# A two-layer decoder trunk on one core: retention transposes held back, output weights laid elsewhere, the start of x reordered

## The chip, the core and the metric

The kernel runs on one core of a Trainium2 chip. The time is that of one execution on the device in microseconds (us), the median of several executions. TensorE is called PE here, VectorE DVE, ScalarE ACT, GpSimd POOL and SyncE SP; nearly all transfers are issued by SP.

## The reference

The trunk has two layers over a sequence of 2048 rows with 1024 columns. Each layer is `x <- x + RMSNorm_post(mixer(RMSNorm_pre(x)))`. The mixer of layer 0 feeds one input projection to retention (4 heads, chunks of 128 rows, rotary q and k) and to stick-breaking attention (8 heads); the mixer of layer 1 feeds HGRN2 (4 heads) and an RG-LRU behind a causal convolution. Each path is multiplied by its own SiLU gate, the two are put side by side, and one output projection follows. The part of retention that the change touches is, for a chunk:

```
scores = einsum('bhnid,bhnjd->bhnij', qc, kc) * decay
o_intra = einsum('bhnij,bhnje->bhnie', scores, vc)
chunk_kv = einsum('bhnjd,hj,bhnje->nbhde', kc, k_decay, vc)
```

and afterwards an RMS norm over each head of `o_intra + o_inter`.

## The kernel before

The sequence is worked in two halves of 1024 rows: layer 0 half 0, layer 0 half 1, layer 1 half 0, layer 1 half 1. Each of these four steps has a mixer (`stick` for layer 0, which contains the retention; `hgrn` for layer 1, which contains the LRU), and an `out_phase` that multiplies the mixed columns by `w_out`, adds x and prepares the transposed input of the next step. The place where a mixer's last projection ends on PE and the first matmul of `out_phase` begins is called a seam here. There are four seams; in the profiled execution they lie near 505, 1260, 1720 and 2189 us.

Every float32 matmul with 512 columns is made of three products of a high and a low part: a weight piece `raw` is loaded by SP, ACT casts it to `wh` (`load_w`, L131), DVE takes the rest to `wl` (L132), and PE multiplies (wh, xh), (wh, xl) and (wl, xh). `w_out` of one column half (`c`) comes in four such pieces, q0 to q3, of two row blocks each. The mixed columns of half a sequence are written to memory (`mixd`) by the mixers, except the last 512 wide block of each of the two groups `g` of 512 rows, which goes straight to the tiles `mh` and `ml` (`mix_direct`, L218 and L219). The stored ones come back as one tile `mr` for each of eight blocks of 128 rows (`mix_rows`, load L225), which ACT casts to `mh` (L227) and DVE to `ml` (L228). The block with number 0 is called row 0, and so on.

In `stick` the last work before the seam is `ret_gate` for head 3, once for g=0 and once for g=1: 24 matmuls into a PSUM tile `pp`, a sigmoid `sg` on ACT (L296), and the two products on DVE, L297 (`ro` times `sg`) and L298 (times `pp`). In `hgrn` the last work is `lg_proj(3)`, likewise with a sigmoid (L198) and two products on DVE (L204, L777).

The retention of one chunk runs as side work between other matmuls (`weave` and `mixed` deal out matmuls by nanoseconds that the generators yield). Its steps on PE are the scores (L328), the transposes of k (L334), the products with v and the state (L344, L345), the k-v products (L350), and at the end four transposes of the normed result `rst` (L361), which need `rs`, a root computed by POOL (L71), and DVE's product L357. `late` with `later`, `tick` and `flush` is a list of postponed functions with due times in nanoseconds of PE work.

Each engine works through its own list of instructions in the order in which the program gives them to it, after the scheduler's priorities; a tile that takes over memory of an older tile waits for the older one's last reader.

## Time and profile before

| | |
|---|---|
| median of 3 runs | 2286.71 us (2285.96 to 2290.03) |
| profiled execution | 2291.48 us, of which the span of its instructions is 2289.6 us |
| PE | 97% of the span busy |
| DVE, ACT, POOL | 61%, 48%, 31% |
| PE before its first matmul | 9.39 us |

The span is the time from the first to the last instruction on the core. A line of the timeline gives the start, the duration, the engine, the line of the kernel and what is written from what, and in brackets how long the engine had been idle before and what ended that. Matmuls overlap: their listed duration is about 0.39 us, while they start 0.227 us apart when nothing is waited for.

### The profile page before, as it was taken

The page shows a single profiled execution, that of the slowest core. Times are in us where ns is not written, and L with a number is a line of the kernel's source. Part 1 is how long each engine was busy: PE and PEld are TensorE (multiplying, and loading weights), DVE is VectorE, ACT ScalarE, POOL GpSimd, SP SyncE. Part 2 cuts the span into 40 slices and gives each one's busy share as a digit, 9 for nine tenths or more (in the row PEclk, how much of TensorE's full clock was granted, in tenths as well). Part 3 has the DMA queues.
Part 4 walks back from the last instruction along what each step waited for, and adds up shares of the span by engine and source line. Part 5 has one row for each costly group of instructions (what it writes and reads, how often), then busy time and mean ns, then how long its engine had stood idle before and what let it go on. Part 6 is the DMA issues. An engine that isn't in the chain of part 4 may idle for free.

```text
span 2289.6 us, 31620 instructions
## 1 busy us (share of the span) xinstructions
PE 2213.7 (97%) x11392; PEld 1805.6 (79%) x11392; DVE 1390.7 (61%) x2049; ACT 1099.4 (48%) x2192; POOL 706.0 (31%) x992
## 2 busy tenths in 40 slices
PE   7999999999999999999999999999999999999998
PEld 6888877777888888788777887877877877878777
DVE  5545567674567677888898554655555535455543
ACT  5334456553455666777776433243245323433331
POOL 0322244421044344665664001222240013122300
PEclk9999999999999999999999999999999999999999
DMA  6443334246433222213323641111116511111161
GB/s 191 112 124 97 111 104 120 86 132 208 160 103 104 65 74 79 79 50 91 88 58 103 213 151 38 42 38 37 52 50 212 190 47 33 42 37 42 51 221 74
DMA packets 236092, 223.69 MB, mean 98 GB/s; under 512 B 21280, under 2 KB 181408, under 8 KB 235936
## 3 DMA queue, kind: packets, MB, share of 16 engines
q1 hardware_dynamic: 235776, 221.15, 31.4%
q8 instruction: 90, 1.47, 0.3%
q14 instruction: 66, 0.54, 0.1%
q0 software_dynamic: 160, 0.52, 0.1%
HBM read 148.22 MB, written 52.43 MB: 88 GB/s over the span
## 4 chain that ended last, share of the span: by engine, by line
PE 78%; DVE 10%; ACT 4%; DMA 3%; issue 3%; POOL 2%; SPq 0%; POOLq 0%; DVEq 0%; ACTq 0%
PE pp L152 42%; PE pp L640 5%; PE o L640 4%; PE o L515 4%; PE z L640 4%; PE tr L500 4%; PE z L474 2%; DVE a L487 2%; PE z L473 2%; PE z L894 2%; PE tr L112 1%; DMA xr<-in_x 1%; PE z L747 1%; DVE wl L132 1%; DVE wtl L505 1%
## 5 line engine op out<-in xcount | busy, mean ns | idle before, releaser
L152 PE MATMUL pp<-xh,wh 128*128 128x512 f32 x1664 | 687.5, 413 | 0.6 <-ACT xh L114 0.6
L152 PE MATMUL pp<-xh,wl 128*128 128x512 f32 x1664 | 658.1, 396 | 0.0
L152 PE MATMUL pp<-xl,wh 128*128 128x512 f32 x1664 | 656.5, 395 | 0.0
L152 PEld LDWEIGHTS pp<-xh,wl 128*128 128x128 f32 x1664 | 313.4, 188 | 67.7 <-issue 1.4
L490 POOL TENSOR_TENSOR b<-b,a 128x511 f32<-128x511 f32 (+2 forms) x320 | 316.2, 988 | 161.9 <-DVE a L487 96.1
L152 PEld LDWEIGHTS pp<-xh,wh 128*128 128x128 f32 x1664 | 314.3, 189 | 53.9 <-ACT xh L114 1.0
L152 PEld LDWEIGHTS pp<-xl,wh 128*128 128x128 f32 x1664 | 315.1, 189 | 49.3 <-issue 0.5
L487 DVE TENSOR_TENSOR_SCAN a<-a,past 128x512 f32<-128x512 f32 x192 | 244.5, 1275 | 76.6 <-ACT a L477 74.4
L477 ACT ACTIVATE a<-z 128x512 f32<-128x512 f32 (+2 forms) x320 | 172.4, 539 | 235.7 <-PE z L474 197.1
L132 DVE TENSOR_TENSOR wl<-raw,wh 128x1024 fp32r<-128x1024 f32 x136 | 171.1, 1264 | 141.9 <-ACT wh L131 139.6
L131 ACT CAST wh<-raw 128x1024 fp32r<-128x1024 f32 x136 | 142.8, 1053 | 194.1 <-PE pp L152 168.2
L71 POOL TENSOR_TENSOR rs<-rs,mhalf 128x1 f32<-128x1 f32 (+1 forms) x96 | 67.0, 698 | 515.3 <-DVE rs L70 506.6
L505 DVE TENSOR_TENSOR wtl<-tr,wth 128x512 fp32r<-128x512 f32 (+1 forms) x320 | 190.1, 595 | 39.0 <-ACT wth L504 38.0
L504 ACT CAST wth<-tr 128x512 fp32r<-128x512 f32 (+1 forms) x320 | 169.5, 530 | 62.9 <-PE tr L500 61.0
L500 PE MATMUL tr<-ident,b 128*128 128x128 f32 x1088 | 176.1, 276 | 11.8 <-DVE wtl L505 10.7
L500 PEld LDWEIGHTS tr<-ident,b 128*128 128x128 f32 x1088 | 133.5, 141 | 59.1 <-DVE wtl L505 17.6
L478 ACT ACTIVATE b<-z 128x512 f32<-128x512 f32 (+2 forms) x320 | 171.0, 534 | 0.0
L482 DVE TENSOR_TENSOR_SCAN a<-a,past 128x128 f32<-128x128 f32 (+3 forms) x128 | 104.5, 817 | 85.0 <-ACT a L477 84.6
L515 PE MATMUL o<-wth,v 128*128 128x512 f32 (+1 forms) x320 | 128.1, 400 | 0.2 <-ACT mol L521 0.2
L866 POOL TENSOR_TENSOR kg<-kg,t 128x256 f32<-128x256 f32 x96 | 71.1, 740 | 173.2 <-PE z L894 108.0
L480 POOL TENSOR_SCALAR_AFFINE_SELECT b<-b 128x128 f32<-128x128 f32 x128 | 44.2, 345 | 259.6 <-ACT b L478 251.2
L473 PE MATMUL z<-k,qh 128*128 128x512 f32 (+2 forms) x320 | 118.6, 371 | 1.3 <-DMA k<-kd 0.6
(216 smaller groups left out, 3610.3 us busy)
## 6 DMA issues: line engine op xcount, KB each, us to landing
raw<-in_even_w_in SPq DMA_DIRECT2D x56, 512.0 KB, 3.9
raw<-in_odd_w_in SPq DMA_DIRECT2D x48, 512.0 KB, 3.8
xr<-in_x SPq DMA_DIRECT2D x32, 512.0 KB, 4.2
xr<-x1d SPq DMA_DIRECT2D x32, 512.0 KB, 4.5
mr<-mixd SPq DMA_DIRECT2D x32, 448.0 KB, 4.8
qh<-qrh SPq DMA_DIRECT2D x64, 128.0 KB, 2.3
ql<-qrl SPq DMA_DIRECT2D x64, 128.0 KB, 2.4
x1d<-y SPq DMA_DIRECT2D x16, 512.0 KB, 2.9
```

What stands on the lines that cost most here:

```text
L132: nc.vector.tensor_tensor(out=wl, in0=raw, in1=wh.bitcast(F32), op=ALU.subtract)
L152: nc.tensor.matmul(ps, w[:, k, :], xx[g][:, k, :], start=(n == 0), stop=(n == 3 * KD - 1))
L473: nc.tensor.matmul(z[:, 0:n], qh[:, tcol], K[e, c][:, 0:n], start=True, stop=False)
L477: nc.scalar.activation(out=A[:, 0:n], in_=z[:, 0:n], func=AF.Sigmoid, scale=-0.125)
L478: nc.scalar.activation(out=B[:, 0:n], in_=z[:, 0:n], func=AF.Sigmoid, scale=0.125)
L487: nc.vector.tensor_tensor_scan(out=A[:, ::-1], data0=A[:, ::-1], data1=past[:, 0:1].to_broadcast([128, 512]), initial=carry[ti][:, 0:1], o ...
L490: nc.gpsimd.tensor_tensor(out=B[:, 0:n - 1], in0=B[:, 0:n - 1], in1=A[:, 1:n], op=ALU.mult)
L500: nc.tensor.transpose(tr[:, ti * 128:ti * 128 + 128], bt[ti][:, sj * 128:sj * 128 + 128], ident)
L504: nc.scalar.copy(out=wh[:, cols], in_=tr[:, cols])
L505: nc.vector.tensor_tensor(out=wl[:, cols], in0=tr[:, cols], in1=wh[:, cols].bitcast(F32), op=ALU.subtract)
L515: nc.tensor.matmul(O[:, cols], V[e, c][:, sj, :], w[:, cols], start=(diag and sj == 0 and w is wh), stop=(c == 0 and sj == 3 and w is wl))
L640: nc.tensor.matmul(ps, m[g][:, k, o:o + 128], w[:, k % 2, :], start=(n == 0), stop=(n == 3 * KD - 1))
```

## The change

Five parts, in the order of the diff:

1. The `tick` of the list `late` runs any entry that is due, not only the first. The four transposes at the end of a retention chunk, the copy behind them and the store of `ro` are packed into a function `turn`. It is called right behind the scores of the next chunk, or when 9000 ns of PE work have passed, whichever comes first; after the last chunk of a call, at once.
2. At the start of the program row block 0 of x is loaded first, then the identity, then row blocks 1 to 3, then the norm weights; the constant tile `past` is built after the projections of the first pair.
3. Row 0 of the mixed columns of layer 1 is no longer loaded through the weight tiles `raw` ahead of the others, but through the two buffers `mr` of the pool `o2`, as the others.
4. The first two pieces of `w_out` (q0, q1) get a pool of their own, `w2a`, on the other end of the on-chip memory. In layer 1 the LRU's scratch pool `lru1` is given up before `lg_proj(3)`, and the pieces are loaded there; in layer 0 the pool is opened in `out_phase`. The pool `w2` has two buffers where it had four.
5. POOL's product of gate and convolution in the LRU (L755) is made in two halves of 512 columns.

```diff
@@ -22,8 +22,9 @@
 KD = D // 128
 EPS = 1e-6
 LAG = 2
+RET_LAG = 9000
 SHIFT = 1
-EARLY = (0, 1)
+EARLY = (0, 0)
 LEVELS = (2, 4, 8, 16, 32, 64)
 
 
@@ -48,10 +49,7 @@
         return (o_bank[-1] if tag == "o" else ps_p).tile([128, 512], F32, tag=tag, name=tag)
 
     ident = const.tile([128, 128], F32, name="ident")
-    nc.sync.dma_start(out=ident, in_=a["c_ident"])
     pre_w = const.tile([128, 2, KD], F32, name="pre_w")
-    for i in range(2):
-        nc.sync.dma_start(out=pre_w[:, i, :], in_=a["pre_norm_w"][i].rearrange("(k p) -> p k", p=128))
     mhalf = const.tile([128, 4], F32, name="mhalf")
     nc.vector.memset(mhalf, -0.5)
     state = const.tile([128, 512], F32, name="state")
@@ -162,8 +160,9 @@
     def tick(ns):
         for item in late:
             item[0] -= ns
-        while late and late[0][0] <= 0:
-            late.pop(0)[1]()
+        for item in [i for i in late if i[0] <= 0]:
+            late.remove(item)
+            item[1]()
 
     def run(gen):
         for ns in gen:
@@ -315,6 +314,12 @@
         lo, hi = slice(0, 64), slice(64, 128)
         nc.gpsimd.memset(q[hi, 0], 0.0)
         nc.gpsimd.memset(q[lo, 1], 0.0)
+        held = []
+
+        def release():
+            if held:
+                held.pop()()
+
         for ch in chunks:
             gg, o = half * 2 + ch // 4, (ch % 4) * 128
             v = p.tile([128, 4, 128], F32, tag="rv", bufs=2, name="rv")
@@ -327,6 +332,7 @@
             for h in range(4):
                 nc.tensor.matmul(sc[:, h, :], k[:, h // 2, :], q[:, h % 2, h // 2, :], start=True, stop=True)
             yield 860
+            release()
             st = p.tile([128, 4, 128], F32, tag="rst", name="rst")
             nc.vector.tensor_tensor(out=st, in0=sc, in1=decay, op=ALU.mult)
             ktp = bank("tr")
@@ -355,14 +361,18 @@
                                                in1=kvp[:, pr, :], op0=ALU.mult, op1=ALU.add)
             rs = rms_heads([st[:, h, :] for h in range(4)], kt[:, 0:128], 4)
             nc.vector.tensor_tensor(out=st, in0=st, in1=rs.unsqueeze(2).to_broadcast([128, 4, 128]), op=ALU.mult)
-            yield 0
-            pt = bank("tr").rearrange("p (h t) -> p h t", h=4)
-            for h in range(4):
-                nc.tensor.transpose(pt[:, h, :], st[:, h, :], ident)
+
+            def turn(st=st, gg=gg, o=o):
+                pt = bank("tr").rearrange("p (h t) -> p h t", h=4)
+                for h in range(4):
+                    nc.tensor.transpose(pt[:, h, :], st[:, h, :], ident)
+                ot = t_p.tile([128, 4, 128], F32, tag="sg", name="rot")
+                nc.scalar.copy(out=ot, in_=pt)
+                nc.sync.dma_start(out=rod[gg][:, :, o:o + 128], in_=ot)
+            held.append(turn)
+            later(RET_LAG, lambda turn=turn: release() if held and held[0] is turn else None)
             yield 440
-            ot = t_p.tile([128, 4, 128], F32, tag="sg", name="rot")
-            nc.scalar.copy(out=ot, in_=pt)
-            nc.sync.dma_start(out=rod[gg][:, :, o:o + 128], in_=ot)
+        release()
 
     kd = [[dr_p.tile([128, 512], F32, name=f"kd{h}_{c}") for c in range(2)] for h in range(8)]
     vd = [[dr_p.tile([128, 512], F32, name=f"vd{h}_{c}") for c in range(2)] for h in range(8)]
@@ -372,11 +382,6 @@
             kv_p, qr_p, q_p, a_p, b_p, wt_p, g_p, t_p, r_p = (scope(es, n, b) for n, b in (
                 ("skv", 8), ("sqr", 2), ("sq", 2), ("sa", 6), ("sb", 9), ("swt", 3), ("sg", 3), ("stmp", 2), ("srt", 1)))
             past = scope_o(es, 1).tile([128, 512], F32, tag="past", name="past")
-            build = t_p.tile([128, 512], F32, tag="sg", name="build")
-            nc.vector.memset(build, 0.0)
-            nc.gpsimd.affine_select(out=build[:, 384:512], in_=build[:, 384:512], compare_op=ALU.is_gt, fill=1.0,
-                                    base=0, pattern=[[-1, 128]], channel_multiplier=1)
-            nc.scalar.copy(out=past, in_=build)
             D_ = [({}, {}, {}, {}) for _ in range(4)]
 
             def pair_proj(pr):
@@ -552,6 +557,11 @@
             t_att = 65000 if half else 23000
             cs = rope_tables(half, r_p)
             run(pair_proj(0))
+            build = t_p.tile([128, 512], F32, tag="sg", name="build")
+            nc.vector.memset(build, 0.0)
+            nc.gpsimd.affine_select(out=build[:, 384:512], in_=build[:, 384:512], compare_op=ALU.is_gt, fill=1.0,
+                                    base=0, pattern=[[-1, 128]], channel_multiplier=1)
+            nc.scalar.copy(out=past, in_=build)
             flush()
             def qk(*parts):
                 return ret_proj_qk(half, xT, r_p, t_p, cs, parts)
@@ -574,11 +584,27 @@
             weave(att(3), t_att, seq(side((5, 8), proj_of(1, pair_gate(3))), gate(0, 1)), 43500)
             run(gate(2, 3))
 
-    def out_phase(layer, half, M, following):
+    def piece(layer, c, q, pool):
+        order = (0, 1, 2, 4, 5, 6, 7, 3) if layer == 0 else tuple(range(8))
+        return load_w(w_out[layer][:, c * 512:(c + 1) * 512], 2, 512, pool, order[2 * q:2 * q + 2])
+
+    class first_pieces:
+        def __init__(self, layer, es, instead=None):
+            self.layer, self.es, self.instead = layer, es, instead
+
+        def __iter__(self):
+            if self.instead:
+                proj_w(1, 2560 + 3 * 128)
+                self.instead.close()
+            self.pool = scope(self.es, "w2a", 2, side="right")
+            self.made = [piece(self.layer, 0, q, self.pool) for q in range(2)]
+            return iter(())
+
+    def out_phase(layer, half, M, following, ahead, first):
         prep_row = prep_step = xT = None
         with ExitStack() as es:
             scope_o(es, 2)
-            w2_p, p2, p1, y_p = scope(es, "w2", 4), scope(es, "o2", 2), scope(es, "o1", 1), scope(es, "y", 8)
+            p2, w2_p, p1, y_p = scope(es, "o2", 2), scope(es, "w2", 2), scope(es, "o1", 1), scope(es, "y", 8)
             if following:
                 rows, prep_row, x_p = prep_rows(es, *following)
                 xT, prep_step = prep_cols(rows, following[0])
@@ -587,13 +613,12 @@
             early = EARLY[layer]
             mrs = [None] * early
             mh, ml = zip(*(mix_slot(M, g) for g in range(2)))
-            order = (0, 1, 2, 4, 5, 6, 7, 3) if layer == 0 else tuple(range(8))
-
-            def piece(c, q, pool):
-                return load_w(w_out[layer][:, c * 512:(c + 1) * 512], 2, 512, pool, order[2 * q:2 * q + 2])
-
+            if not first:
+                first = first_pieces(layer, ahead)
+                with tc.high_priority(offset=300):
+                    iter(first)
             with tc.high_priority(offset=300):
-                W = [[piece(0, q, w2_p) for q in range(4)], []]
+                W = [first.made + [piece(layer, 0, q, w2_p) for q in (2, 3)], []]
             with tc.high_priority(offset=300):
                 for tt in range(early, 8):
                     mrs.append(mix_rows(half, M, tt, p2, "mr"))
@@ -626,11 +651,11 @@
                 if c == 1:
                     if not prep_step:
                         xrs.update((tt, load_x(tt)) for tt in range(8))
-                    W[1] += [piece(1, q, w2_p) for q in (2, 3)]
+                    W[1] += [piece(layer, 1, q, first.pool) for q in (2, 3)]
                 for tt in range(8):
                     if (c, tt) == (0, 2):
                         with tc.issue_after(mrs[5]):
-                            W[1] += [piece(1, q, w_p) for q in (0, 1)]
+                            W[1] += [piece(layer, 1, q, w_p) for q in (0, 1)]
                     g, o = tt // 4, (tt % 4) * 128
                     ps = bank(("pp", "z", "o")[(c * 8 + tt) % 3])
                     n = 0
@@ -752,7 +777,8 @@
                     nc.scalar.activation(out=av, in_=r, func=AF.Exp, scale=lam8[:, j:j + 1])
                     nc.scalar.activation(out=r, in_=r, func=AF.Tanh, scale=lam4[:, j:j + 1])
                     nc.scalar.activation(out=r, in_=r, func=AF.Sqrt)
-                    nc.gpsimd.tensor_tensor(out=ig, in0=ig, in1=xc, op=ALU.mult)
+                    for x in (slice(0, 512), slice(512, 1024)):
+                        nc.gpsimd.tensor_tensor(out=ig[:, x], in0=ig[:, x], in1=xc[:, x], op=ALU.mult)
                     nc.vector.scalar_tensor_tensor(out=r, in0=av, scalar=1.0, in1=r, op0=ALU.add, op1=ALU.mult)
                     if half == 0:
                         nc.vector.memset(r[:, 0:1], 1.0)
@@ -784,9 +810,10 @@
 
         return lx_proj, lg_proj
 
-    def hgrn(es, half, xT, M):
+    def hgrn(es, half, xT, M, ahead):
         scope_o(es, 2)
-        lp1, lp5, lpg = scope(es, "lru1", 1), scope(es, "lru5", 4), scope(es, "lrug", 1)
+        scratch = ExitStack()
+        lp1, lp5, lpg = scope(scratch, "lru1", 1, side="right"), scope(es, "lru5", 4), scope(es, "lrug", 1)
         p1, p, p4 = scope(es, "hg1", 1), scope(es, "hg", 2), scope(es, "hg4", 4)
         ones = p1.tile([128, 128], F32, name="ones")
         nc.vector.memset(ones, 1.0)
@@ -931,8 +958,10 @@
         flush()
         for h in range(3):
             weave(head_scan(h), 20000, seq(head_proj(h + 1), lx_proj(h + 1)), 57000)
-        weave(head_scan(3), 20000, seq(*(lg_proj(j) for j in range(4))), 41600)
+        pieces = first_pieces(1, ahead, scratch)
+        weave(head_scan(3), 20000, seq(*(lg_proj(j) for j in range(3)), pieces, lg_proj(3)), 41600)
         flush()
+        return pieces
 
     steps = [(layer, half) for layer in range(2) for half in range(2)]
     with ExitStack() as es:
@@ -940,6 +969,11 @@
         xT, step = prep_cols(rows, 0)
         for tt in range(8):
             row(tt)
+            if tt == 0:
+                nc.sync.dma_start(out=ident, in_=a["c_ident"])
+            if tt == 3:
+                for i in range(2):
+                    nc.sync.dma_start(out=pre_w[:, i, :], in_=a["pre_norm_w"][i].rearrange("(k p) -> p k", p=128))
             if tt in (3, 5):
                 proj_w(0, 2048 if tt == 3 else 2560)
             if tt % 4 == 3:
@@ -947,6 +981,7 @@
                     step(tt // 4, k)
     for n, (layer, half) in enumerate(steps):
         M = {}
+        ahead, first = ExitStack(), None
         if layer == 0:
             stick(half, xT, M)
             if half == 1:
@@ -954,8 +989,9 @@
                 odd_const()
         else:
             with ExitStack() as es:
-                hgrn(es, half, xT, M)
-        xT = out_phase(layer, half, M, steps[n + 1] if n + 1 < len(steps) else None)
+                first = hgrn(es, half, xT, M, ahead)
+        with ahead:
+            xT = out_phase(layer, half, M, steps[n + 1] if n + 1 < len(steps) else None, ahead, first)
 
 
 def _tables():
```

In the pieces of the two programs' orders below, the numbers of lines are those of each program: L131 before is L129 after, L227 is L226, L218 is L217, L296 is L295, L361 is L368, L152 is L150, L198 is L197.

ACT at the first seam of layer 0, before. `wh<-raw` are the casts of weight pieces (first x2: q0, q1; second: q2, q3), `mh<-mr` the casts of rows, `sg<-pp` the sigmoids of `ret_gate`, the last two those of head 3, for g=0 and for g=1:

```order
L131 CAST wh<-raw 128x1024 x2
L520 COPY mo<-o 64x512
L521 COPY mol<-o 64x512
L296 ACTIVATE sg<-pp 128x512 x2
L131 CAST wh<-raw 128x1024 x2
L296 ACTIVATE sg<-pp 128x512
L227 CAST mh<-mr 128x7x128
L218 CAST mh<-ro 128x512
L227 CAST mh<-mr 128x7x128
L296 ACTIVATE sg<-pp 128x512
L227 CAST mh<-mr 128x7x128
L218 CAST mh<-ro 128x512
```

The same place after the change:

```order
L295 ACTIVATE sg<-pp 128x512 x2
L226 CAST mh<-mr 128x7x128 x2
L295 ACTIVATE sg<-pp 128x512
L217 CAST mh<-ro 128x512
L226 CAST mh<-mr 128x7x128
L295 ACTIVATE sg<-pp 128x512
L226 CAST mh<-mr 128x7x128
L129 CAST wh<-raw 128x1024 x2
L217 CAST mh<-ro 128x512
L226 CAST mh<-mr 128x7x128 x2
L129 CAST wh<-raw 128x1024 x2
L226 CAST mh<-mr 128x7x128 x2
```

All four casts of weights stood ahead of the sigmoid of head 3 for g=0 and of the rows; now they stand behind the sigmoid for g=1, q0 and q1 behind row 3, and q2 and q3 behind rows 4 and 5. In the new program the cast of q0 also waits for DVE's product with that last sigmoid (the tile `sg` lay in memory that `w2a` takes over), and PE's fourth matmul of `out_phase`, which is the first of a fourth row block, for the product after it (L298 before); the loads of `raw` for q2 and q3 stand on SP behind the loads of rows 4 and 5 and wait for `wl` of q0 and q1, whose `raw` tiles they take over.

PE at the second chunk of the retention in half 0, from the attention's product that stands 2 instructions ahead of the transposes `tr<-ident,rst` before:

```order
L152 MATMUL pp<-xl,wh 128x512
L152 MATMUL pp<-xh,wl 128x512
L473 MATMUL z<-k,qh 128x256
L474 MATMUL z<-k,ql 128x256
L361 MATMUL tr<-ident,rst 128x128 x4
L152 MATMUL pp<-xh,wh 128x512
L152 MATMUL pp<-xl,wh 128x512
L152 MATMUL pp<-xh,wl 128x512
```

The same place after the change:

```order
L478 MATMUL z<-k,qh 128x256
L479 MATMUL z<-k,ql 128x256
L150 MATMUL pp<-xh,wh 128x512
L150 MATMUL pp<-xl,wh 128x512
L150 MATMUL pp<-xh,wl 128x512
L505 MATMUL tr<-ident,b 128x128 x4
L150 MATMUL pp<-xh,wh 128x512
L150 MATMUL pp<-xl,wh 128x512
L150 MATMUL pp<-xh,wl 128x512
L368 MATMUL tr<-ident,rst 128x128 x4
L520 MATMUL o<-wth,v 128x512
```

The transposes have moved behind six projection matmuls and one set of the attention's transposes.

ACT at the first seam of layer 1, before. `mh<-gt` are the direct casts of the LRU's last gate for g=0 and g=1:

```order
L198 ACTIVATE sg<-pp 128x512
L227 CAST mh<-mr 128x7x128
L218 CAST mh<-gt 128x512
L198 ACTIVATE sg<-pp 128x512
L131 CAST wh<-raw 128x1024 x2
L218 CAST mh<-gt 128x512
L131 CAST wh<-raw 128x1024 x2
L227 CAST mh<-mr 128x7x128 x2
L643 ACTIVATE y,sy<-pp 128x512
```

The same place after the change:

```order
L197 ACTIVATE sg<-pp 128x512
L217 CAST mh<-gt 128x512
L197 ACTIVATE sg<-pp 128x512
L217 CAST mh<-gt 128x512
L129 CAST wh<-raw 128x1024 x2
L226 CAST mh<-mr 128x7x128 x4
L668 ACTIVATE y,sy<-pp 128x512
```

Row 0, which was cast ahead of the gate, now stands behind the last gate's cast and the pieces q2 and q3; q0 and q1 are cast earlier and are out of this piece.

## Rows read from the trace of the kernel before

**Rows 1.** The page, part 1: busy us, share of the span, instructions.
```profile
PE 2213.7 (97%) x11392; PEld 1805.6 (79%) x11392; DVE 1390.7 (61%) x2049; ACT 1099.4 (48%) x2192; POOL 706.0 (31%) x992
```

**Rows 2.** Waits of PE: line, releaser: us in total, times, longest.
```profile
...
PE tr L361 <- DVE rst L357: 12.6, 8, 2.3
...
PE pp L640 <- ACT wh L131: 5.5, 4, 1.9
PE z L894 <- POOL kg L866: 5.2, 10, 0.7
PE pp L640 <- DVE wl L132: 4.1, 5, 1.2
PE tr L361 <- DVE wtl L505: 3.8, 5, 2.0
```

**Rows 3.** Timeline of PE, last retention chunk of each sequence half.
```profile
...
436.63 0.63 PE L361 MATMUL tr<-ident,rst 128*128 128x128 f32 x4 [1.09 <-DVE rst L357]
...
1169.80 0.63 PE L361 MATMUL tr<-ident,rst 128*128 128x128 f32 x4 [2.11 <-DVE rst L357]
```

**Rows 4.** Windows: stretch, length, busy by engine, PEclk (1.00 full), DMA share, GB/s.
```profile
...
263.60:267.00 3.40, 3.40 (x11) 2.77 (x10) 0.17 (x1) 1.07 (x2) 0.00 (x0) 0.51 0.10 33
...
1728.00:1734.80 6.80, 6.05 (x14) 4.63 (x15) 4.22 (x5) 3.61 (x5) 0.00 (x0) 0.50 0.75 234
```

**Rows 5.** Timeline of ACT: the first row block of x at the start.
```profile
...
6.58 1.06 ACT L97 ACTIVATE xn<-xr 128x1024 f32<-128x1024 f32 x1 [4.50 <-DMA xr<-in_x]
```

**Rows 6.** Timeline of ACT at the first layer-0 seam.
```profile
...
495.74 1.05 ACT L131 CAST wh<-raw 128x1024 fp32r<-128x1024 f32 x1 [0.65 <-DMA raw<-in_even_w_out]
...
504.12 0.94 ACT L227 CAST mh<-mr 128x896 fp32r<-128x896 f32 x1 [4.22 <-DMA mr<-mixd]
...
506.36 0.59 ACT L296 ACTIVATE sg<-pp 128x512 f32<-128x512 f32 x1
509.85 0.94 ACT L227 CAST mh<-mr 128x896 fp32r<-128x896 f32 x1 [2.89 <-DMA mr<-mixd]
```

**Rows 7.** Timeline of DVE at the same seam.
```profile
...
495.13 1.23 DVE L132 TENSOR_TENSOR wl<-raw,wh 128x1024 fp32r<-128x1024 f32 x1 [0.25 <-ACT wh L131]
...
505.09 1.09 DVE L228 TENSOR_TENSOR ml<-mr,mh 128x896 fp32r<-128x896 f32 x1 [3.74 <-ACT mh L227]
...
507.70 0.69 DVE L297 TENSOR_TENSOR ro<-ro,sg 128x512 f32<-128x512 f32 x1
```

**Rows 8.** Timeline of SP's DMA issues at the same seam.
```profile
...
497.40 1.51 SPq L225 DMA_DIRECT2D mr<-mixd  x2
...
506.21 8.85 SPq L225 DMA_DIRECT2D mr<-mixd  x4
```

**Rows 9.** Timeline of PE at the same seam.
```profile
...
505.11 0.50 PE L640 MATMUL pp<-wh,mh 128*128 128x512 f32 x1 [0.40 <-ACT mh L227]
```

**Rows 10.** DMA issues over the whole run: count, KB each, median us to landing.
```profile
...
mr<-mixd SPq DMA_DIRECT2D x32, 448.0 KB, 4.8
...
raw<-in_even_w_out SPq DMA_DIRECT2D x8, 512.0 KB, 5.6
...
mixd<-ro SPq DMA_DIRECT2D x12, 256.0 KB, 2.0
```

**Rows 11.** Timeline of DVE, end of the constants before the second seam.
```profile
...
1251.47 0.16 DVE L712 TENSOR_SCALAR lam<-s 128x4 f32<-128x4 f32 x1
```

**Rows 12.** Timeline of PE at the second layer-0 seam.
```profile
...
1260.21 0.39 PE L640 MATMUL pp<-wh,mh 128*128 128x512 f32 x1
```

**Rows 13.** Timeline of PE at the first layer-1 seam.
```profile
...
1721.08 0.49 PE L640 MATMUL pp<-wh,mh 128*128 128x512 f32 x1 [1.62 <-ACT wh L131]
```

**Rows 14.** Timeline of ACT at the same seam.
```profile
...
1719.50 0.60 ACT L198 ACTIVATE sg<-pp 128x512 f32<-128x512 f32 x1 [3.21 <-PE pp L152]
...
1722.09 0.61 ACT L218 CAST mh<-gt 128x512 fp32r<-128x512 f32 x1
```

**Rows 15.** Timeline of DVE at the same seam.
```profile
...
1720.85 0.69 DVE L777 TENSOR_TENSOR gt<-gt,ht 128x512 f32<-128x512 f32 x1
```

## The prediction

> **What bounds the kernel now.** I read the shares of the engines first: PE is busy 97% of the span [rows 1], so that of 2289.6 us some 76 are idle on PE, and everything else can only matter through them. Then I read what ended PE's waits [rows 2]: the transposes at the end of a retention chunk wait 12.6 us for DVE's `rst` and 3.8 us for a free `tr` bank, the first matmuls of `out_phase` wait 5.5 and 4.1 us for weights, and the HGRN's products 5.2 us for POOL. Then the granted clock in short windows: behind a wait of 2.1 us it stands at 0.51, its lower level of 1.2 GHz, for 3.4 us, and behind the longer waits of the first layer-1 seam at 0.50 for 6.8 us [rows 4]. What PE does there takes twice as long, so a stretch of 3.4 us costs 1.7. Three such stretches follow the retention's waits (one row of them stands in [rows 4]), 6.8 + 3.4 us follow the layer-1 seams. Last I read the seams engine by engine. At layer 0 PE loses almost nothing: 0.40 us before the first matmul [rows 9], nothing at the second seam, where the start at 1260.21 has no wait [rows 12]. At layer 1 all 5.5 + 4.1 us of the weight waits are lost, 1.62 of them before the first matmul [rows 13].
>
> The sum is made against the profiled execution: 2291.5 us, 1.9 of it outside the span. It is 4.8 above the median of the runs, to which I carry the difference over.
>
> **Retention.** The eight `rst` waits are 2.1, 0.7, 2.3, 1.1, 1.1, 1.2, 2.0 and 2.1 us long, 12.6 together. In the new order I counted the matmuls between a chunk's k-v products and its transposes (0.227 us for 512 columns): six of the eight places gain 0.9 to 2.0 us of work. The last chunk of each half gains none, since `release` is called there at once; its 1.1 and 2.1 stay [rows 3]. What the cover leaves of the others is 0.3, 0, 0.7, 0, 0.3 and 0, so 4.5 of 12.6 stays. The `tr` waits (3.8, five times) come from a bank whose last reader is an attention cast. The new position has such a neighbour as often as the old one, so I let half of it stay, 1.9. A new wait: `rst` has one buffer, so that DVE's score product of the next chunk now waits for the held transposes, and on DVE the attention's scans and `wtl` stand behind it. PE needs this product 0.6 to 1.4 us of matmuls after the transposes; the product takes 0.69, as its like in [rows 7], and two handovers. I put 2.0 us for all sixteen chunks (bounds 0, where the cover is enough, and 6, 0.4 each). Idle: -8.1 - 1.9 + 2.0 = -8. Of the three slow stretches I count two as gone, -3.3. Together -11; bounds -18 (all but the last chunks' waits gone, three stretches) and -4.
>
> **Start.** The first square of x ends ACT's wait of 4.50 us for the load [rows 5]. Three small loads stood ahead of it on SP; two issues take 1.51 us in [rows 8], so up to 2.2 us, and I take -1.5 (bounds -0.5 and -2.2). The norm weights are needed only behind PE's first transposes, which is their cover. The copy to `past` leaves ACT's chain of the first rows; that is within this bound.
>
> **Gate product in halves.** Of the ten waits for `kg` [rows 2] only those right behind an L755 could change. In the first LRU block both halves still stand together ahead of `kg`; in the others one half has moved two or three short products forward. 0, bounds -2 and +0.5.
>
> **Layer-0 seams.** This is the largest term. Before, all four weight casts were done (the last began at 495.74 [rows 6]) before PE came to the seam at 505.11 - 0.40 = 504.7. Now PE's first matmul waits for the cast of q0, which stands on ACT behind rows 0 to 3 and the last sigmoid, and waits for DVE's product with that sigmoid; the sigmoid needs PE's last matmul. In order, with a row's load at its median of 4.8 us [rows 10], ACT's row cast 0.94, sigmoid 0.59, weight cast 1.05 [rows 6], DVE's row 1.09, product 0.69, weight 1.23 [rows 7]:
> - Rows 0 and 1 were issued at 497.40 and the first was cast at 504.12, 6.7 us later. The weight pieces that shared the queue are loaded earlier now, so that the store ahead of them can land at its median of 2.0 [rows 10]; I put the issue at 496.0. Row 0 is cast 500.8 to 501.7, row 1 to 502.7, the sigmoid of g=0 to 503.3, its products on DVE to 504.7, `mh<-ro` to 505.3.
> - Row 2's load waits for DVE's row 0 (502.8), lands at 507.6, its cast ends at 508.5; then the last sigmoid, 509.1; on DVE row 2 to 509.6 and the product to 510.3. The cast of q0 runs 510.3 to 511.35. Stall 6.65.
> - After four matmuls PE needs `wl` of q0, behind DVE's row 3 and second product: 513.3, a stall of 1.0.
> - Only then is the `raw` tile free for q2; its load takes 5.6 [rows 10], the cast ends at 520.0, and PE's work with q0 and q1 up to there is 15 matmuls, 3.4 us: a stall of 3.35.
>
> 11.0 us, less the 0.4 of before. At the second seam rows 0 and 1 also wait for the tile in which the LRU's constants end at 1251.6 [rows 11], while the seam is at 1260.2: the same steps give a cast of q0 that ends at 1267.05, stalls of 6.85 + 1.0 + 3.35 = 11.2, where there was none. Each seam gets 2.5 us for the clock (between one stretch, 1.7, and the 6.8 us of [rows 4], 3.4). Together +26. Lower bound: rows in time, so that only sigmoid, product and cast stand between (2.5), 0.3 for `wl`, and q2 with a load of 3.6 (509.85 less 506.21, [rows 6, 8]) leaves 1.3: 4.1 + 1.7 each, +11. Upper bound: every load at 6.7, which gives 15 + 3.4 each, +36.
>
> Here a page of the Trainium skill stands against the rows. DMA: Bandwidth & Descriptors, section "Anatomy of one DMA — SWDGE (gpsimd) path", fits a transfer as about 2.0 us and its bytes at 436 GB/s, which is 3.05 us for a row's 448 KB and 3.2 for a weight piece, as estimates from that page. Its fit is for GpSimd's path; the rows here, on SP's queue, have 4.8 and 5.6 in the median and 3.6 at the least. By the page a seam would stall some 5 us instead of 11, and the whole sum would come out near 2293.
>
> **Layer-1 seams.** The weight waits go, since q0 and q1 are cast before `lg_proj(3)`. But row 0 now stands on ACT behind the last gate's cast, q2 and q3. PE ends at 1721.08 - 1.62 = 1719.46 [rows 13]; sigmoid to 1720.1 and `mh<-gt` after it [rows 14], which waits for DVE's second product, 1721.5 [rows 15]; so `mh<-gt` to 1722.15, q2 and q3 to 1724.25, row 0 to 1725.2: a stall of 5.75. Row 1's load waits for the same product and lands at 1726.4, cast to 1727.3; PE's third matmul needs it, 1.65 more. 7.4 at each of the two, 14.8 against 9.6 before: +5.2. The clock lost 3.4 + 1.7 there and will lose about 2.5 at each: 0. Together +5, bounds +1 and +8.
>
> **Sum.** -11 - 1.5 + 0 + 26 + 5 = +18.5: 2310 for a profiled execution, 2305 for the median.
>
> **Rivals.**
> - *Rows in time (not slower).* If the mixed rows and q2 come as fast as the 3.6 us of the shortest row, the layer-0 seams cost the lower bound, +11. The place is the cast of q0; with the retention as above the sum is +3.5, 2290, and with the retention at its best -3, 2283. It decides from the point at which a layer-0 seam costs under 6 us with its clock: then the sum is within 4.6 us of none. For it: the weight loads leave the queue before the seam. Against: rows 0 and 1 took 6.7 us, and row 2 cannot be asked for before row 0 is split.
> - *The retention's wait only moves.* DVE stands at the held transposes, and what is behind it comes late: attention transposes wait instead. The gain is 0 to -3, and the time 2313 to 2316. For it: the score product now waits for PE in most chunks. Against: DVE is busy 61% only [rows 1].
> - *The casts are early in effect.* PE's last matmuls at the layer-0 seam hide more than I see, or the change gains elsewhere what I do not count: 2275. The written order speaks against it: the first matmul of `out_phase` cannot start before PE's own last matmul has gone through ACT, DVE and ACT.
>
> **How the numbers follow.** Forecast 0.65; rows in time 0.18 (two thirds of it within 0.2%); the wait that moves 0.10; early in effect 0.07. A measurement of this kernel tells about 0.2%, 4.6 us, from no change. Faster (under 2282): 0.06 + 0.07 = 0.13. Same: 0.12. Slower: 0.75. The range leaves out the third rival and the far ends of the bounds: 2284 to 2321. The forecast's own range is 2294 to 2316.
>
> **What would show it.** PE's waits at the layer-0 seams: `pp L665 <- ACT wh L129`, some 6 us twice, then for `wl` and for q2, with the lower clock behind them; if these are under 3 us, the seam term is wrong. `tr L368 <- DVE rst` should fall from 12.6 to 4 to 5 us with the two last chunks in it; if it stays above 9 or waits for DVE's score product appear in its stead, the retention term is. At layer 1 the first matmul should wait near 5.7 us for `mh` and not for `wh`; the first matmul of the program should come near 7.9 instead of 9.39.

## The result and the profile after

The changed kernel takes 2301.62 us (median of 4 runs, 2300.39 to 2304.11) against 2286.97 us of the kernel before (2285.96 to 2290.03): ratio 1.0065, 95% interval 1.005 to 1.008, so 14.65 us slower. The forecast was 2305, its own range 2294 to 2316. The sign and the main mechanism were right; the largest term was too large.

The shares of the engines in the changed kernel (page, part 1) hardly differ from [rows 1]; the span is 2300.9 us:

```profile
PE 2216.9 (96%) x11392; PEld 1806.7 (79%) x11392; DVE 1395.1 (61%) x2049; ACT 1101.1 (48%) x2192; POOL 707.9 (31%) x1000
```

PE's waits after the change, as in [rows 2] (us in total, times, longest). L665 is the matmul of `out_phase`, L129 the cast of weights, L226 the cast of a row, L340 the transposes of k, L368 the held transposes, and L510 is where DVE empties a `tr` bank for the attention:

```profile
PE pp L665 <- ACT wh L129: 12.1, 4, 5.4
...
PE pp L665 <- ACT mh L226: 11.0, 2, 5.5
PE tr L340 <- DVE wtl L510: 4.5, 6, 1.6
PE tr L368 <- DVE rst L363: 3.8, 3, 2.1
...
PE tr L368 <- DVE wtl L510: 3.0, 1, 3.0
```

The retention's wait fell from 12.6 to 3.8 us, and the seams' waits grew from 5.5 + 4.1 to 12.1 + 11.0. The timeline of PE has one large wait at each seam (in brackets the idle time before and what ended it). Here are both seams of layer 0, where [rows 9, 12] had 0.40 and none, and the first of layer 1, where [rows 13] had 1.62:

```profile
504.93 0.79 PE L665 MATMUL pp<-wh,mh 128*128 128x512 f32 x1 [5.00 <-ACT wh L129]
...
506.84 0.79 PE L665 MATMUL pp<-wl,mh 128*128 128x512 f32 x1
...
513.66 0.50 PE L665 MATMUL pp<-wh,mh 128*128 128x512 f32 x1 [1.25 <-ACT wh L129]
...
1265.84 0.80 PE L665 MATMUL pp<-wh,mh 128*128 128x512 f32 x1 [5.45 <-ACT wh L129]
1273.85 0.50 PE L665 MATMUL pp<-wh,mh 128*128 128x512 f32 x1 [0.44 <-ACT wh L129]
...
1735.88 0.80 PE L665 MATMUL pp<-wh,mh 128*128 128x512 f32 x1 [5.52 <-ACT mh L226]
1737.30 0.79 PE L665 MATMUL z<-wh,mh 128*128 128x512 f32 x1 [0.20 <-ACT mh L226]
```

Windows of the stretches with the lower granted clock in the changed kernel (columns as in [rows 4]: the number behind the length is the time that PE is busy in the stretch): three in the mixers of layer 0, then the two layer-0 seams and the two layer-1 seams. In the half microsecond just ahead of each seam's stretch, and in that just behind it, the granted clock is 1.00:

```profile
398.18:401.59 3.41, 3.07 (x15) 3.08 (x15) 0.94 (x2) 0.21 (x1) 1.53 (x4) 0.50 0.12 35
1128.63:1132.04 3.41, 3.17 (x15) 2.64 (x14) 2.93 (x5) 1.32 (x3) 1.50 (x3) 0.50 0.63 165
1169.59:1173.00 3.41, 3.41 (x12) 2.93 (x12) 3.20 (x4) 1.88 (x4) 1.96 (x3) 0.50 0.60 157
503.99:510.82 6.83, 5.89 (x13) 4.30 (x14) 5.87 (x7) 4.23 (x5) 0.00 (x0) 0.50 0.82 217
1265.16:1271.99 6.83, 6.16 (x14) 4.54 (x15) 6.09 (x7) 3.97 (x5) 0.00 (x0) 0.50 0.83 238
1732.79:1739.61 6.82, 3.53 (x8) 2.33 (x9) 5.05 (x5) 3.98 (x5) 0.00 (x0) 0.50 0.52 169
2200.41:2207.24 6.83, 3.81 (x8) 2.62 (x9) 5.05 (x5) 3.68 (x5) 0.00 (x0) 0.50 0.58 185
```

At 0.50 half of PE's busy time in a stretch is lost: 2.9 and 3.1 us at the layer-0 seams, 1.8 and 1.9 at the layer-1 seams. By the rows the first layer-0 seam costs 5.00 + 1.25 + 2.9 = 9.2 us and the second 5.45 + 0.44 + 3.1 = 9.0, together 18.2 (17.8 less the 0.4 of before) where the prediction had 26.

ACT at the first layer-0 seam shows why, beside [rows 6]:

```profile
495.17 0.95 ACT L226 CAST mh<-mr 128x896 fp32r<-128x896 f32 x1 [5.49 <-DMA mr<-mixd]
496.43 0.95 ACT L226 CAST mh<-mr 128x896 fp32r<-128x896 f32 x1 [0.32 <-DMA mr<-mixd]
...
501.06 0.94 ACT L226 CAST mh<-mr 128x896 fp32r<-128x896 f32 x1 [0.58 <-DMA mr<-mixd]
501.91 0.59 ACT L295 ACTIVATE sg<-pp 128x512 f32<-128x512 f32 x1
502.99 0.94 ACT L226 CAST mh<-mr 128x896 fp32r<-128x896 f32 x1 [0.49 <-DMA mr<-mixd]
503.83 1.99 ACT L129 CAST wh<-raw 128x1024 fp32r<-128x1024 f32 x2
...
512.57 1.04 ACT L129 CAST wh<-raw 128x1024 fp32r<-128x1024 f32 x1 [2.12 <-DMA raw<-in_even_w_out]
```

The chain is the one foreseen: rows 0 to 3 and the last sigmoid, then the casts of q0 and q1 at 503.83. PE's last matmul ends at 504.93 - 5.00 = 499.93 here, so that all of it is to be counted from there: row 2 is cast 1.1 us behind that end where the forecast had 2.9 (507.6 against 504.7), and q0 3.9 us behind it, right after row 3, where the forecast had 5.6. The loads of rows 2 and 3 went out at 497.27, as SP's issues show, beside [rows 8]:

```profile
497.27 8.33 SPq L224 DMA_DIRECT2D mr<-mixd  x4
506.81 1.96 SPq L125 DMA_DIRECT2D raw<-in_even_w_out  x3
```

Row 2 was thus cast 3.8 us after its issue. The medians from issue to landing over the whole run (page, part 6) are shorter too than in [rows 10]:

```profile
mr<-mixd SPq DMA_DIRECT2D x32, 448.0 KB, 4.3
...
raw<-in_even_w_out SPq DMA_DIRECT2D x8, 512.0 KB, 4.5
```

At layer 1 ACT stands as forecast (`mh<-gt`, then both casts of weights, then row 0):

```profile
1732.48 0.62 ACT L217 CAST mh<-gt 128x512 fp32r<-128x512 f32 x1 [1.48 <-DVE gt L803]
1733.00 1.99 ACT L129 CAST wh<-raw 128x1024 fp32r<-128x1024 f32 x2
1734.90 0.93 ACT L226 CAST mh<-mr 128x896 fp32r<-128x896 f32 x1
1736.31 0.94 ACT L226 CAST mh<-mr 128x896 fp32r<-128x896 f32 x1 [0.48 <-DMA mr<-mixd]
```

### The profile page after: what moved, and what is told of

Its sections match the earlier page's. It is cut to its first block, busy times and chain, and to the rows that moved or that the text cites. A ratio compares the mean times of both kernels' runs of the same rounds, so it can differ in the third digit from the quotient of the medians.

```text
span 2300.9 us, 31603 instructions
## 1 busy us (share of the span) xinstructions
PE 2216.9 (96%) x11392; PEld 1806.7 (79%) x11392; DVE 1395.1 (61%) x2049; ACT 1101.1 (48%) x2192; POOL 707.9 (31%) x1000
## 4 chain that ended last, share of the span: by engine, by line
PE 82%; DVE 8%; ACT 3%; DMA 3%; issue 2%; POOL 2%; SPq 0%; POOLq 0%; DVEq 0%; ACTq 0%
PE pp L150 43%; PE pp L665 6%; PE o L665 5%; PE z L665 5%; PE o L520 4%; PE tr L505 4%; PE z L479 2%; PE z L478 2%; DVE a L492 2%; PE z L921 2%; PE tr L110 1%; PE z L772 1%; DMA mr<-mixd 1%; DVE wtl L510 1%; POOL kg L893 1%
## 5 line engine op out<-in xcount | busy, mean ns | idle before, releaser
L150 PE MATMUL pp<-xh,wh 128*128 128x512 f32 x1664 | 687.2, 413 | 0.0
L150 PE MATMUL pp<-xh,wl 128*128 128x512 f32 x1664 | 656.9, 395 | 0.0
L150 PE MATMUL pp<-xl,wh 128*128 128x512 f32 x1664 | 655.3, 394 | 0.0
L150 PEld LDWEIGHTS pp<-xh,wl 128*128 128x128 f32 x1664 | 312.8, 188 | 68.2 <-issue 1.4
L150 PEld LDWEIGHTS pp<-xh,wh 128*128 128x128 f32 x1664 | 314.1, 189 | 52.7 <-issue 1.0
L150 PEld LDWEIGHTS pp<-xl,wh 128*128 128x128 f32 x1664 | 314.4, 189 | 48.9 <-issue 0.5
L129 ACT CAST wh<-raw 128x1024 fp32r<-128x1024 f32 x136 | 142.7, 1052 | 187.6 <-PE pp L150 165.8
L510 DVE TENSOR_TENSOR wtl<-tr,wth 128x512 fp32r<-128x512 f32 (+1 forms) x320 | 189.8, 594 | 41.6 <-ACT wth L509 40.7
L520 PE MATMUL o<-wtl,v 128*128 128x512 f32 (+1 forms) x320 | 117.8, 368 | 0.0
```

What stands on the lines that cost most here:

```text
L150: nc.tensor.matmul(ps, w[:, k, :], xx[g][:, k, :], start=(n == 0), stop=(n == 3 * KD - 1))
L510: nc.vector.tensor_tensor(out=wl[:, cols], in0=tr[:, cols], in1=wh[:, cols].bitcast(F32), op=ALU.subtract)
L520: nc.tensor.matmul(O[:, cols], V[e, c][:, sj, :], w[:, cols], start=(diag and sj == 0 and w is wh), stop=(c == 0 and sj == 3 and w is wl))
```

## The experiments

Each ratio is to the kernel before on the same chip, with its 95% interval; the median of the kernel before on that chip stands beside each time. Gains and losses in us are the ratio's difference times 2287. The numbers of lines in the rows are those of each kernel.

**One part alone: the held transposes** (the kernel before with part 1 of the change and nothing else; the diff is that of `tick` and of the retention).

> The kernel before with the held retention transposes alone. By the traces it gains 5.9 us in half 0 and 1.9 us in half 1: 2279 from 2287, with the waits for the normed product down from 12.6 to about 4 us. Forecast of the prediction: a gain of 11, 2276. Rival, the wait only moves to the attention's transposes and to the score product: 2285 to 2288.

Measured: 2279.47 us beside 2286.98, 0.9962 (0.9949 to 0.9974), -8.7 us (-11.7 to -5.9; the two medians are 7.5 apart). Waits of PE, first for the transposes of k in the kernel before, then in this kernel:

```profile
PE tr L334 <- DVE wtl L505: 2.8, 4, 1.4
```

```profile
PE tr L343 <- DVE wtl L518: 4.7, 6, 1.6
PE tr L371 <- DVE rst L366: 3.8, 3, 2.1
...
PE tr L371 <- DVE wtl L518: 3.0, 1, 3.0
...
PE pp L353 <- DVE rst L340: 0.8, 1, 0.8
```

The rival that the wait only moves, with a gain of 0 to 3 us, is out: 8.8 us of `rst` waits went, 0.8 came at the next chunk's products for its score product, and the transposes of k wait 4.7 us in place of 2.8.

**One part alone: the start** (part 2).

> The kernel before with the new order of loads at the start alone (and the constant tile built later). By the trace of the changed kernel the first matmuls come later and 1.4 us are lost: 2288.4, with the first PE matmul near 10.4 us. The prediction's term was a gain of 1.5: 2285.5, first matmul near 7.9 us.

Measured: 2285.29 us beside 2286.98, 0.9995 (0.9986 to 1.0004): -1 us, not told from none.

**One part alone: the halves of the gate product** (part 5).

> The kernel before with POOL's gate product in two halves alone. The waits of PE for POOL's products fell from 5.2 to 2.7 us in the changed kernel; if the halves did it, the time falls by 2.5 us to 2284.5 and the waits are near 2.7 here too. The prediction's term was 0: 2287, waits near 5.2, and then another part of the change did it.

Measured: 2287.3 us beside 2286.98, 1.0000 (0.9991 to 1.0009): nothing, as forecast. Its `kg` waits are 2.5 us against the 5.2 of [rows 2], without any effect on the time:

```profile
PE z L895 <- POOL kg L867: 2.5, 10, 0.4
```

Without the halves they are 2.5 in two of the kernels of these experiments (held transposes alone, start alone) and 3.7 in a third (norm weights behind row 0), all with the LRU of before. So the halves aren't what lowers them. That the 5.2 belongs to the one profiled execution of before is likely, but not shown, since there is no second profile of that kernel.

**The norm weights behind row 0** instead of row 3, in the kernel before with the start changed:

```diff
-            if tt == 3:
+            if tt == 0:
                 for i in range(2):
                     nc.sync.dma_start(out=pre_w[:, i, :], ...)
```

> The kernel before with the first row of x, the identity and the norm weights issued in this order, the other rows behind them. In the changed start two issues of the norm weights took 3.9 us of SP behind four loads of x and the first weight piece was asked for at 7.1 instead of 4.4 us. If that is what ate the gain of the earlier first row, the time is 1.5 us under the kernel before, 2285.5, and the first projection starts before 15 us. Rival: rows 1 to 3 set the start whatever the order: 2287.

Measured: 2288.61 us beside 2289.44, 0.9994 (0.9984 to 1.0003): the same as the other order within the intervals.

**Layer 0's weights back in one pool of four**, behind the row buffers; the rest of the change stays.

```diff
-            p2, w2_p, p1, y_p = scope(es, "o2", 2), scope(es, "w2", 2), scope(es, "o1", 1), scope(es, "y", 8)
+            p2, w2_p, p1, y_p = scope(es, "o2", 2), scope(es, "w2", 2 if first else 4), scope(es, "o1", 1), scope(es, "y", 8)
...
-            if not first:
-                first = first_pieces(layer, ahead)
-                with tc.high_priority(offset=300):
-                    iter(first)
...
-                W = [first.made + [piece(layer, 0, q, w2_p) for q in (2, 3)], []]
+                W = [(first.made if first else []) + [piece(layer, 0, q, w2_p) for q in ((2, 3) if first else range(4))], []]
...
```

> The changed kernel with the weight pieces of layer 0's output projection back in one pool of four buffers, allocated behind the row buffers. If the layer-0 seams cost what the two traces say (7.0 and 10.7 us between the same matmuls of both kernels, with the slow clock), the time falls from 2301.6 by 17 to 18 us to 2284, and PE's waits of 5.0 and 5.45 us for the cast of q0 vanish. Rival: the loss comes from the order of the row buffers and the weights' buffers in memory, which stays as in the changed kernel; then the seams keep most of it and the time is 2296 to 2302.

Measured: 2290.57 us beside 2286.98, 1.0013 (1.0004 to 1.0022): 11.9 us less than the changed kernel, but not all that was expected. The first layer-0 seam is clean; at the second PE waits for the first mixed rows (timeline of PE in this kernel):

```profile
1252.90 0.50 PE L661 MATMUL pp<-wh,mh 128*128 128x512 f32 x1 [3.01 <-ACT mh L226]
1254.33 0.80 PE L661 MATMUL z<-wh,mh 128*128 128x512 f32 x1 [0.50 <-ACT mh L226]
```

SP issues those rows at 1247.74 only. What it waited for ahead of them is the last of DVE's LRU constants, `lam`, which ends at 1247.67 (waits of SP in this kernel):

```profile
SPq L224 <- DVE lam L733: 4.3, 1, 4.3
```

So the rows wait for the memory of the LRU's constants, as the prediction had it; the next kernel asks whether that is all of the loss.

**The same with the pools of layer 0 also in their old order**, weights ahead of rows:

```diff
-            p2, w2_p, p1, y_p = scope(es, "o2", 2), scope(es, "w2", 2), scope(es, "o1", 1), scope(es, "y", 8)
+            if first:
+                p2, w2_p = scope(es, "o2", 2), scope(es, "w2", 2)
+            else:
+                w2_p, p2 = scope(es, "w2", 4), scope(es, "o2", 2)
+            p1, y_p = scope(es, "o1", 1), scope(es, "y", 8)
...
```

> The changed kernel with layer 0's output weights fully as before: one pool of four buffers, allocated ahead of the row buffers. With the rows' buffers behind the weights' the loads of rows 0 and 1 at the second seam no longer wait for the memory of the LRU's constants. Theory, two causes at that seam (weights' place and rows' place): its remaining loss of 9 us goes and the time is 2281 to 2283 against 2290.6 with the weights' place alone undone. Rival, the rest of the loss at that seam comes from the held retention or the LRU's constants themselves: it stays near 2290.

Measured: 2283.42 us beside 2289.44 for before on that chip, 0.9979 (0.9969 to 0.9988). The wait at the second seam is gone, another 7.8 us: the rows' place in memory was the second cause there.

**Only the order of the pools turned round**, with the place of their own for q0 and q1 kept, in both layers:

```diff
-            p2, w2_p, p1, y_p = scope(es, "o2", 2), scope(es, "w2", 2), scope(es, "o1", 1), scope(es, "y", 8)
+            w2_p, p2, p1, y_p = scope(es, "w2", 2), scope(es, "o2", 2), scope(es, "o1", 1), scope(es, "y", 8)
```

> The changed kernel with the pool of the weight pieces opened ahead of the pool of the mixed rows; the separate place of q0 and q1 stays. What is asked: do the two causes at the second layer-0 seam add up? Theory 1, they add: the rows' place cost 7.8 us in the pair of kernels that both had the weights back in one pool, so the same is given back here: ratio to the kernel before 1.003, 2294 us, and the first matmul of the second seam waits for nothing over 2 us. Theory 2, they overlap: the cast of q0 then still stands behind the last sigmoid and its product, so the second seam becomes like the first, which cost 7.4 by the traces against 10.5: a gain of 3 us, ratio 1.005, 2298.5 us, and both seams wait about 5 us for the weight cast. I hold theory 2 for likelier.

Measured: 2314.14 us beside 2289.13, 1.0107 (1.0091 to 1.0123): 9.6 us slower than the changed kernel, which neither theory expected. PE in this kernel at the second layer-0 seam and the first of layer 1, then the load of row 0 on SP at that layer-1 seam and what SP waited for ahead of it, and the same load in the changed kernel:

```profile
1265.55 0.79 PE L665 MATMUL pp<-wh,mh 128*128 128x512 f32 x1 [4.68 <-ACT wh L129]
1274.11 0.50 PE L665 MATMUL pp<-wh,mh 128*128 128x512 f32 x1 [2.33 <-ACT wh L129]
...
1740.64 0.80 PE L665 MATMUL pp<-wh,mh 128*128 128x512 f32 x1 [9.97 <-ACT mh L226]
```

```profile
1735.76 1.26 SPq L224 DMA_DIRECT2D mr<-mixd  x2
```

```profile
SPq L224 <- DVE ml L218: 14.8, 1, 14.8
```

```profile
1718.89 14.13 SPq L224 DMA_DIRECT2D mr<-mixd  x2
```

At layer 0 the turn gives nothing back: 4.68 + 2.33 stands in place of 5.45 + 0.44. So the two causes at the second seam overlap, and each suffices for a stall; this much of theory 2 is borne out, its gain of 3 us is not. At layer 1 the rows now lie in memory that comes free with the last gate's low part (`ml`, L218): their load goes out at 1735.76, where in the changed kernel row 0's went out at 1718.89, and the seam waits 9.97 us instead of 5.52, 4.45 more; the other layer-1 seam is the same, since the two waits together are 20.0 us instead of 11.0. So the order of the pools in the change is the better one for layer 1; at layer 0 it costs 7.8 us where all four pieces lie in one pool, and nothing where q0 and q1 have their own.

**Row 0 of layer 1 loaded ahead again**, in the changed kernel: `EARLY = (0, 1)`.

> The changed kernel with row 0 of layer 1's mixed columns loaded ahead of the others again, as before. Theory: at both layer-1 seams the wait of 5.5 us for the cast of row 0 goes, PE works on row 0 (24 matmuls, 5.4 us) while ACT casts q2 and q3, and each seam loses 2 us instead of 5.7 plus part of a slow stretch: 2290 to 2295 from 2301.6. Rival: the waits move to q2, q3 and row 1, which stand on ACT as late as before: 2299 to 2303.

Measured: 2293.97 us beside 2289.44, 1.0019 (1.0010 to 1.0028), some 10.5 us less than the changed kernel. With `EARLY = (0, 0)` the change brings the pieces forward and loses the gain to the row.

**The layer-1 part alone**, on the kernel before, first with `EARLY = (0, 0)`:

> The kernel before with the layer-1 part of the change alone: scratch given up early, q0 and q1 cast ahead of the last gate, all rows of layer 1 through the row buffers. The prediction's term is +5 (bounds 1 to 8): 2292 us, ratio 1.0022, with waits of some 5.5 us for row 0 at each of the two layer-1 seams and none for q0. The sum of the other parts leaves +5.0, so the same. Rival: the remainder hid an error of other parts, and the layer-1 part costs nothing (ratio 1.000) or the full 7.4 us a seam with its clock (ratio 1.006).

Measured: 2291.29 us beside 2289.13, 1.0011 (1.0001 to 1.0020), +2.5 us. Then with `EARLY = (0, 1)`:

> The same with row 0 of the mixed columns of layer 1 loaded ahead through a weight tile, as before the change. If row 0's place in ACT's order is all that the layer-1 part loses, the early pieces now show their gain: the waits of 5.5 and 4.1 us of the kernel before shrink to 3.4 in all and two stretches of the lower clock go, some -6 to -8 us: 2280 us, ratio 0.997. Rival: the pieces bring nothing even so, because the row and the pieces share ACT: ratio 1.000.

Measured: 2281.28 us beside 2289.13, 0.9968 (0.9958 to 0.9979), -7.3 us. Waits of PE in this kernel at the layer-1 seams, the two together:

```profile
PE pp L655 <- ACT wh L131: 1.9, 2, 0.9
PE pp L655 <- DVE wl L132: 1.5, 2, 0.8
```

**What is good put together**: held transposes, halves, early pieces in layer 1 with row 0 ahead, layer 0's weights as before, norm weights behind row 0.

> A version put together: held retention transposes, layer 0's output weights as before, layer 1's first pieces early and its row 0 early as well, the norm weights behind the first row of x. Sum of the parts by the runs so far: -7.5 for the retention, -1 to -2 for the start, and at each layer-1 seam some 5 us less than before (waits of 4.8 and a slow stretch of 1.7 to 3.4 against about 2): 2268 to 2274. If the layer-1 waits only move to q2 and q3, 2277 to 2280.

Measured: 2272.18 us beside 2289.44, 0.9927 (0.9912 to 0.9942): 16.7 us faster than before and some 32 faster than the change as it was made.

## Why the prediction was right, and where it was off

**The sign and the cause.** The layer-0 seams were named as what makes the kernel slower, with the wait `pp L665 <- ACT wh L129` as its mark, and the runs show it: with that part undone in full the rest is 0.9979. "Rows in time" had a part in it, since row 2 took 3.8 us and not 4.8; but its point, a seam under 6 us with its clock, was not reached (9.2 and 9.0). That the time came out within 4 us of the forecast is in part luck: the two seam terms were some 9 us too large together, and the retention's gain was 2.3 too large the other way.

**Layer-0 seams: +26 forecast, +19.7 measured** (11.9 and then 7.8, by the two undoings, some 4 us either way by the intervals of their ratios; 17.8 by the rows of the profile). The parts that the prediction gives add up to 26.8 and not to 26. This is the term that was mis-sized, in three places:
- *Rows and q0.* From the end of PE's last matmul to PE's first one the forecast had 6.65 and 6.85; the waits are 5.00 and 5.45. Row 2's load was issued 2.7 us ahead of PE's end where I had 1.9, and took 3.8 us where I had 4.8. The product with the last sigmoid was then done in time, and the cast of q0 stood only behind row 3's.
- *`wl` of q0.* The forecast stall of 1.0 is not there: the matmul with `wl` at 506.84 has no wait in its brackets. PE ran at half clock at that moment, so the four matmuls ahead of it took 1.9 us where 0.9 was counted, and covered DVE's work. Clock and wait were added up as if they were independent; they cover each other.
- *q2.* 3.35 forecast, 1.25 and 0.44 measured, at the first seam for the same reason: from `wl` to the end of q2's cast it took 6.8 us (506.84 to 512.57 + 1.04) where the forecast had 6.65, but PE's fifteen matmuls of that time lasted 5.6 us and not 3.4, most of them at half clock. At the second seam the load was shorter too (1267.72 to 1272.75, against 506.81 to 512.57). How much is covered is not the same each time: the kernel with `EARLY = (0, 1)`, whose layer 0 is the same, waits 2.07 and 3.15 us here.

The clock itself was nearly right: 2.5 forecast for each seam, 2.9 and 3.1 measured. The page "DMA: Bandwidth & Descriptors" of the Trainium skill (section "Anatomy of one DMA — SWDGE (gpsimd) path") would have a row in 3.05 us, an estimate by its fit for GpSimd's path. For SP's queue that is not borne out here: the median of a row is 4.3 and of a weight piece 4.5; no run has these loads on GpSimd's path. The sum of 2293 by that fit lay farther from the result than mine.

For the second seam I gave one mechanism for both causes, and the runs say how they stand: with q0's own place the rows' late memory costs nothing more, without it 7.8 us by itself (3 us either way).

**Retention: -11 forecast, -8.7 measured.** The count of the cover was good: 4.5 us of `rst` waits were to stay, 3.8 did, with the last chunks' 1.09 and 2.09 in it, as forecast. The `tr` waits were to halve to 1.9; one of 3.02 us is left. The score product's wait at the one `rst` buffer was put at 2.0, and 0.8 shows, but the transposes of k wait 1.9 more for attention's `wtl`, which I had not counted. Idle: -8.8 - 0.8 + 0.8 + 1.9 = -6.9 where the forecast had -8; the remaining 1.8 of 8.7 is left for the clock, which was put at -3.3. The prediction counted three slow stretches in the mixers of layer 0; the profile of before has a fourth, at 400.17. Of four, two are left in the kernel with this part alone (1118.82 and 1159.78, 0.50 for 3.41 us each) and three in the changed kernel. One of these, at 1128.63, is new and follows the wait of 3.02 us of the held transposes themselves. So the clock gave back 1.9 to 3.5 us in these profiles, and as the kernel with the halves alone, whose retention is that of before, has three such stretches, a closer split is not shown.

**Start: -1.5 forecast, -1 ± 2 measured.** The step as I put it was wrong all the same: the first row comes sooner (first square of x at 4.46 instead of the 6.58 of [rows 5]), but the first matmul did not come at 7.9. It starts at 10.38 in the changed kernel. The nearest cause is DVE's order: the product of row 0 (L97), which PE needs, now stands behind the mean square of row 1 (L68), and that waits for row 1, which ACT squares at 8.30 only. Timeline of DVE in the changed kernel:

```profile
5.64 0.15 DVE L68 TENSOR_SCALAR rs<-ss 128x1 f32<-128x1 f32 x1 [4.12 <-ACT xn L95]
9.48 0.15 DVE L68 TENSOR_SCALAR rs<-ss 128x1 f32<-128x1 f32 x1 [3.68 <-ACT xn L95]
9.57 0.75 DVE L97 TENSOR_SCALAR xn<-xr,rs 128x1024 f32<-128x1024 f32 x1
```

SP is held up too: behind row 3 the issue of the norm weights' two small loads lasts 3.88 us, so that the first weight piece is asked for at 7.07. Timeline of SP in the changed kernel:

```profile
1.72 1.38 SPq L92 DMA_DIRECT2D xr<-in_x  x3
3.14 3.88 SPq L976 DMA_DIRECT2D pre_w<-in_pre_norm_w  x2
```

In the kernel with these weights behind row 0 the issue takes 1.06 us, DVE's product of row 0 stands ahead of row 1's mean square, and PE's first transposes come at 7.44; but the next ones wait for row 1 (timeline of PE in that kernel):

```profile
7.44 0.69 PE L109 MATMUL tr<-ident,xn 128*128 128x128 f32 x2 [7.44 <-DVE xn L96]
11.94 0.69 PE L109 MATMUL tr<-ident,xn 128*128 128x128 f32 x2 [3.81 <-DVE rs L67]
```

Its second row starts at 11.94; in the changed kernel it starts at 11.57. So 2.9 us at the first row are worth nothing, since PE needs all four rows and the transposes of the fourth start at about the same time, 14.88 and 14.51 (13.81 in the kernel before). I had priced the first row alone.

**Gate product: 0 forecast, 0 measured.**

**Layer-1 seams: +5 forecast, +2.5 measured alone** (0.2 to 4.6). The wait for row 0 was 5.52 for a forecast of 5.75. Row 1's was 0.20 for 1.65: its load went out at 1732.47, behind DVE's second product as foreseen, but was there for ACT 3.8 us later (1736.31), where the forecast had 4.9. The clock, put at no difference, came back a little: PE was busy at half clock for 3.5 and 3.8 us at the two seams, 3.7 lost, where the profile of before lost 4.7. By the rows the part thus comes to 11.0 + 0.4 + 3.7 against 9.6 + 4.7, +0.8. By difference (0.9979 less retention and start) the part would cost 5.0 us; the two agree within their intervals.

**The sum** of the measured parts is -8.7 - 1.1 + 0 + 19.7 + 2.5 = +12.4 against +14.65 measured. The parts have uncertainties of 2 to 4 us each, so that the missing 2 us are within them and no part is named for them.

## What to carry to other kernels

A transfer or cast that is "ahead" on its engine gains only if everything it needs, the memory under it too, is free ahead: ask for each buffer which older tile it takes over and when that tile's last reader is done, and ask it for every step that shares the code, since the same order of pools cost the second layer-0 seam 7.8 us, with the weights in one pool, and spared each layer-1 seam 4.5. When one operand of a matmul is brought forward, look at the other one: the early weight pieces made layer 1 2.5 us slower while row 0 stood behind them, and 7.3 faster with row 0 in its old place. Stalls in a row and the lower clock behind the first of them aren't summed: the slow stretch covers part of the next wait.

## What the hardware showed that I had not expected

- The lower clock lasted 6.8 us at each of the four seams of the changed kernel, but began while PE still waited: 0.9 and 0.7 us ahead of PE's first matmul at layer 0, 3.1 and 2.8 us ahead of it at layer 1. So waits of about the same length (5.00 to 5.52 us) cost 2.9 and 3.1 us of clock at layer 0 and 1.8 and 1.9 at layer 1.
- The same two small loads took 1.06 us to issue on SP behind one row and the identity; behind three rows more they took 3.88 us in the changed kernel and 2.11 in the kernel with the new start alone.
- The waits for `kg` came to 5.2 us in the one profiled execution of before, and to 2.5, 2.5 and 3.7 in single profiles of its variants with unchanged LRU: a single profile can carry some us that another, with the same code there, does not.
